# Seven half-size products for the FFN down projection and for the late gate/up pairs, with folded weights kept in DRAM

## The chip, the cores and the metric

The kernel runs on all 8 cores of one Trainium2 chip. Each core computes half of one of the four sequences, and no core waits for another. The metric is the device time of the slowest core, in microseconds (us). The fast executions of the kernel before took 5716.59 to 5722.73 us, but for one of 5781.71. More than half of the executions on record here (76 of the 126 listed with a state) fell into a slow state, whatever the kernel: the cores of one die, or both, show a lower granted TensorE clock, and the time is up to 20% longer (6875.58 us in the kernel before, with 0.812 to 0.816 on cores 0 to 3 and 0.998 to 0.999 on the others). I compare fast executions with fast ones, and stages with stages on cores at a granted clock of 0.98 or more, unless I say otherwise.

The engines of a core are named as in the profile: PE is TensorE, which runs the matmuls (PEld: its weight loads), DVE is VectorE, ACT is ScalarE, POOL is GpSimd, and SP is SyncE, which only issues DMAs here. PSUM is the memory that matmuls write to; the kernel divides its part of it (`ps`, 4096 float32 columns) into eight banks.

## The reference, cut to what matters

```python
D_MODEL, BATCH, SEQ, DEPTH, D_FF = 1024, 4, 8192, 4, 2816
def swiglu(h, w_gate, w_up, w_down):
    return (jax.nn.silu(h @ w_gate) * (h @ w_up)) @ w_down
def reference(x, ...):
    for i in range(DEPTH):
        h = rmsnorm(x, mix_pre_g[i])
        m = mixer_a(h, ...) if i % 2 == 0 else mixer_b(h, ...)   # gated MLP over chunks / causal pooling
        x = x + rmsnorm(m, mix_post_g[i])
        h = rmsnorm(x, ffn_pre_g[i])
        x = x + rmsnorm(swiglu(h, w_gate[i], w_up[i], w_down[i]), ffn_post_g[i])
    return x
```

Inputs are float32. The FFN, three products of 1024 by 2816 for every token and layer, is most of the work.

## The kernel before: the parts that matter

A core takes its tokens in five tiles (0 to 4). A tile has two halves of 384 to 512 columns (tokens), and goes through eight stages: mixer A, FFN, mixer B, FFN, and the same again for layers 2 and 3. Weights are stationary 128 by 128 blocks in bf16; each is used for one matmul per half. They come in pieces of 1 MB into a ring of six slots (`WR`) and are cast from float32 on the way by DMAs that POOL issues; DMAs that need no cast are issued by SP.

```python
def ffn_head(s, v, pi, pc):              # one gate/up pair (two of 22 feature blocks), one half
    # ... 4 banks of PSUM: (gate, up) x two feature blocks, 8 matmuls of v.n columns into each
    t_act(..., sg, bank(bg), AF.Silu)                                # ACT: silu(gate)
    t_dve(..., e.tensor_tensor(out=o, in0=bank(bu), in1=sg(), op=mult))   # DVE: times up

def chain(v, s, post, gpost, nxt, final=None):   # after a stage: post-norm, residual, next pre-norm
    def mult(fc): ... e.tensor_tensor(out=m, in0=m, in1=r, op=mult)           # m * rsqrt(...)
    def add(fc):  ... e.scalar_tensor_tensor(out=x, in0=m, scalar=g, in1=x)   # x += g * m
                  ... st.add(x)                                              # squares (ACT), sums (DVE)
    # ... eight chunks; then the ones-matmul (PE), rsqrt (ACT), and eight H = x * g * r (DVE)

# the FFN stage
pcs = [Piece(wf_gu[l, q]) for q in range(11)]
for pi in range(11):
    for h in hs:
        ffn_head(s, vout[h], pi, pcs[pi])
tp = [Piece(wf_dn[l, q]) for q in range(6)]
for h in hs2:
    out_proj(s, vlast[h], by_block(tp, NJ), NJ, ...)      # 22 x 8 matmuls of v.n columns
    chain(vlast[h], s, sts[h], ...)
```

`chain`: after the last matmul of a half, a serial string of DVE, ACT and PE operations must end before the next stage can start on that half. While it runs, PE has the other half to work on.

The order of instructions on each engine is fixed when the kernel is built: the program places every task with durations that it assumes, and each engine then runs its list in order. Both profiles show it: the instructions of DVE start in one order on all eight cores (4841 before, 6879 after), though at other times, and so do those of ACT, POOL, SP and PE's weight loads. That placement is a plan and not a measurement.

## Time and profile before

| | before |
|---|---|
| fast executions (same rounds as the changed kernel) | 5722.73, 5722.59, 5722.32 us |
| profiled execution (slowest core) | 5754.8 us |
| matmuls per core | 33311 |
| PE / DVE / ACT busy | 99% / 46% / 42% |

The page of the profile, slowest core: busy time with its share of the span, the traffic to memory, the chain of waits that ended last, and the largest group of instructions (line, engine, operation, out<-in, shape, count | busy us, mean ns | idle before, releaser).

```profile
PE 5696.8 (99%) x33311; PEld 3157.3 (55%) x33311; DVE 2630.8 (46%) x4841; ACT 2432.9 (42%) x5236; POOL 258.7 (4%) x492
...
HBM read 1082.53 MB, written 23.66 MB: 192 GB/s over the span
...
PE 94%; DVE 2%; DMA 1%; ACT 1%; issue 1%; another core or an unknown queue 0%; DVEq 0%; SPq 0%; ACTq 0%; POOLq 0%
...
L499 PE MATMUL ps<-H,WR 128*128 128x384 bf16 (+2 forms) x16640 | 2967.7, 338 | 11.8 <-ACT SQ L480 4.3
```

PE is busy 99% of the span and is 94% of the chain, and its largest group has next to no idle time before it (11.8 us beside 2967.7 busy). Undisturbed matmuls of N columns (128 to 512) start every N/2.4 + 2.5 ns on core 7 (medians of 56 ns at 128 columns, 162 at 384, 216 at 512). So PE bounds the kernel, and what can make it faster is fewer PE columns. (Core 1, the slowest of this profile, is on a die whose granted clock was at 0.81 for 149 to 262 us of the span; core 7, used below, is not, and PE is busy there for 5654.5 us.)

Three stretches of core 7 (an undisturbed die) follow: the first FFN of tile 0, mixer B of tile 1 and the FFN of layer 1 in tile 1. The columns are the stretch, its length, busy us of each engine with the count of instructions, the granted clock, the share of the DMA engines and GB/s.

```profile
core 7: us, PE busy (x) PEld busy (x) DVE busy (x) ACT busy (x) POOL busy (x), PEclk, DMA share, GB/s
164.87:349.34 184.47, 184.22 (x1101) 107.56 (x1100) 71.12 (x135) 62.61 (x126) 8.71 (x17) 1.00 0.70 126
1469.03:1525.31 56.28, 54.97 (x358) 28.20 (x357) 43.34 (x75) 41.41 (x89) 2.11 (x4) 1.00 0.51 93
1525.31:1725.89 200.58, 200.58 (x1062) 103.66 (x1060) 73.56 (x123) 59.05 (x111) 8.96 (x17) 1.00 0.47 85
```

In both FFNs PE is busy from end to end: 184.22 of 184.47 us and 200.58 of 200.58 us. What PE waited for in layers 1 to 3 of that tile (us in total, times, the longest):

```profile
PE ps L499 <- DVE H L641: 1.6, 2, 0.8
```

That is all that is listed in 867 us. What DVE, ACT and the DMA engines do is hidden.

### The profile page before, as it was taken

To read this page: it belongs to the slowest core of one execution; us is meant where nothing else is said; L and a number is where in the kernel's file an instruction comes from. 1 tells how busy PE (TensorE), PEld (TensorE's weight loads), DVE (VectorE), ACT (ScalarE), POOL (GpSimd) and SP (SyncE) were. 2 spreads that over 40 slices of the span, in tenths; PEclk is the share of its full clock that TensorE was granted. 3 is DMA by queue.
4 is the path that set the end of the run, shared out by engine and by line. 5 is a ranking of instruction groups with operands and counts; after the bars stand their busy time and mean duration, and the time that the engine had idled before them with its cause. 6 is when DMAs were issued, how large, how long until landed. Compare 5 with 4: busy or idle time off the path is not lost.

```text
span 5754.8 us, 92936 instructions; the slowest of 8 cores (5714.0 to 5754.8 us)
## 1 busy us (share of the span) xinstructions
PE 5696.8 (99%) x33311; PEld 3157.3 (55%) x33311; DVE 2630.8 (46%) x4841; ACT 2432.9 (42%) x5236; POOL 258.7 (4%) x492
## 2 busy tenths in 40 slices
PE   8999999999999999999999999999999999999999
PEld 4555555555555555555545555555565555555556
DVE  5453536352625454443436253524454444525352
ACT  5352635352525353533354253524534453525252
POOL 0000000000000000000000000000000000000000
PEclk9999999999999999999999999999999999999999
DMA  7856676664445545754544455655554676455544
GB/s 141 141 97 107 114 127 117 123 130 81 80 89 98 96 88 107 142 95 81 93 85 86 91 112 111 122 111 103 103 105 95 119 140 112 89 92 96 107 88 90
DMA packets 131409, 604.39 MB, mean 105 GB/s; under 512 B 12560, under 2 KB 55952, under 8 KB 67600
## 3 DMA queue, kind: packets, MB, share of 16 engines
q0 software_dynamic: 70272, 507.82, 51.1%
q1 hardware_dynamic: 60688, 90.63, 5.2%
q8 instruction: 276, 4.52, 0.3%
q14 instruction: 173, 1.42, 0.1%
HBM read 1082.53 MB, written 23.66 MB: 192 GB/s over the span
## 4 chain that ended last, share of the span: by engine, by line
PE 94%; DVE 2%; DMA 1%; ACT 1%; issue 1%; another core or an unknown queue 0%; DVEq 0%; SPq 0%; ACTq 0%; POOLq 0%
PE ps L499 94%; DMA MS<-xT 1%; DVE ACC L596 1%; DVE H L641 0%; DVE MS L688 0%; DMA WR<-wb_out 0%; ACT RS L622 0%; ACT BIG L480 0%; ACT RS L624 0%; DVE BIG L833 0%; DVE X L694 0%; ACT SQ L480 0%; DVE ACC L593 0%; ACT MS L480 0%; DMA X<-xT 0%
## 5 line engine op out<-in xcount | busy, mean ns | idle before, releaser
L499 PE MATMUL ps<-H,WR 128*128 128x384 bf16 (+2 forms) x16640 | 2967.7, 338 | 11.8 <-ACT SQ L480 4.3
L499 PEld LDWEIGHTS ps<-H,WR 128*128 128x128 bf16 x16640 | 1617.7, 98 | 1254.6 <-issue 24.7
L499 PE MATMUL ps<-BIG,WR 128*128 128x384 bf16 (+4 forms) x11056 | 1941.5, 337 | 2.1
L499 PEld LDWEIGHTS ps<-BIG,WR 128*128 128x128 bf16 x11056 | 1078.4, 98 | 832.8 <-issue 24.2
L750 DVE TENSOR_TENSOR BIG<-ps,SG 128x384 bf16<-128x384 f32 (+2 forms) x880 | 510.0, 585 | 1374.3 <-PE ps L499 1294.7
L480 ACT ACTIVATE SG<-ps 128x384 bf16<-128x384 f32 (+2 forms) x880 | 442.8, 513 | 1553.1 <-PE ps L499 1540.7
L596 DVE TENSOR_TENSOR ACC<-ACC,SQ 128x384 f32<-128x384 f32 (+2 forms) x730 | 428.7, 587 | 770.0 <-ACT SQ L480 706.7
L499 PE MATMUL ps<-WR,H 128*128 128x512 bf16 x3216 | 728.3, 386 | 12.8 <-DVE ACC L596 8.1
L480 ACT ACTIVATE MS<-ps 128x384 f32<-128x384 f32 (+3 forms) x648 | 324.5, 511 | 958.8 <-PE ps L499 947.6
L480 ACT ACTIVATE BIG<-ps 128x512 bf16<-128x512 f32 (+1 forms) x914 | 477.3, 561 | 338.2 <-PE ps L499 335.1
L499 PEld LDWEIGHTS ps<-WR,H 128*128 128x128 bf16 x3216 | 318.5, 99 | 402.7 <-issue 67.7
L688 DVE TENSOR_TENSOR MS<-MS,RS 128x384 f32<-128x384 f32 (+3 forms) x640 | 364.6, 580 | 200.0 <-ACT RS L624 199.9
L641 DVE SCALAR_TENSOR_TENSOR H<-X,GV,RS 128x384 bf16<-128x384 f32 (+2 forms) x576 | 330.0, 643 | 142.8 <-ACT RS L624 142.8
L480 ACT ACTIVATE SQ<-X 128x384 bf16<-128x384 f32 (+2 forms) x576 | 300.5, 549 | 200.9 <-DVE ACC L593 96.6
L694 DVE SCALAR_TENSOR_TENSOR X<-MS,GV,X 128x384 f32<-128x384 f32 (+2 forms) x560 | 354.6, 642 | 0.0
L480 ACT ACTIVATE SQ<-ps 128x384 bf16<-128x384 f32 (+3 forms) x648 | 321.9, 510 | 46.2 <-DVE ACC L596 29.2
L509 POOL DMA_DIRECT2D WR<-wf_gu x220 | 116.1, 528 | 2485.1 <-PE ps L499 2452.6
L593 DVE TENSOR_TENSOR ACC<-SQ 128x384 f32<-128x384 bf16 (+2 forms) x146 | 85.4, 585 | 189.4 <-ACT SQ L480 188.6
L480 ACT ACTIVATE SQ<-BIG 128x512 bf16<-128x512 bf16 x268 | 168.2, 638 | 7.1
L622 ACT ACTIVATE RS<-ps,EPSC 128x384 f32<-128x384 f32 (+2 forms) x152 | 92.6, 609 | 139.2 <-PE ps L499 139.1
L864 DVE SCALAR_TENSOR_TENSOR ACC<-ps,GV,BIAS 128x384 f32<-128x384 f32 (+2 forms) x184 | 107.5, 587 | 57.9 <-PE ps L499 54.8
L480 ACT ACT_TABLE_LOAD x94 | 120.6, 1283 | 19.7 <-PE ps L499 14.1
(63 smaller groups left out, 1555.9 us busy)
## 6 DMA issues: line engine op xcount, KB each, us to landing
WR<-wf_gu POOLq DMA_DIRECT2D x220, 1024.0 KB, 10.5
WR<-wf_dn POOLq DMA_DIRECT2D x120, 1024.0 KB, 9.0
WR<-wa_in POOLq DMA_DIRECT2D x79, 1024.0 KB, 14.3
WR<-wa_out POOLq DMA_DIRECT2D x40, 1024.0 KB, 10.0
WR<-wb_in POOLq DMA_DIRECT2D x20, 1024.0 KB, 10.1
WR<-w_s SPq DMA_DIRECT2D x20, 1024.0 KB, 10.2
yT<-MS SPq DMA_DIRECT2D x56, 192.0 KB, 16.6
X<-xT SPq DMA_DIRECT2D x48, 192.0 KB, 18.5
```

What stands on the lines that cost most here:

```text
L480: return e.activation(out=out() if callable(out) else out, in_=in_() if callable(in_) else in_, func=func, **kw)
L499: return e.matmul(out(), lhsT=lhsT() if callable(lhsT) else lhsT, rhs=rhs() if callable(rhs) else rhs, start=start, stop=stop)
L509: return e.dma_start(out=out() if callable(out) else out, in_=in_)
L593: t_dve(self.prio + (1,), lambda e: e.tensor_tensor(out=acc, in0=o0(), in1=o(), op=ALU.add), [k0, kq], ka, v.n)
L596: d = t_dve(self.prio + (1,), lambda e: e.tensor_tensor(out=acc, in0=acc, in1=o(), op=ALU.add), [kq] + ka, ka, v.n)
L622: t.insts.append((lambda e: e.activation(out=r, in_=bank(b, 0, v.n), func=AF.Ln, bias=EPSC[:]), [b, ("EPSC",)], kr, d_act(v.n)))
L641: t_dve(CH + (s, v.p, 1), lambda e, o=o, a=a, g=g, r=r: e.scalar_tensor_tensor(out=o, in0=a, scalar=g, in1=r, op0=ALU.mult, op1=ALU.mult), ...
L688: t_dve(CH + (s, v.p, 0), lambda e: e.tensor_tensor(out=m, in0=m, in1=r, op=ALU.mult), kf("MS", v, fc) + kr, kf("MS", v, fc), v.n)
L694: t_dve(CH + (s, v.p, 0), lambda e: e.scalar_tensor_tensor(out=o, in0=m, scalar=g, in1=x, op0=ALU.mult, op1=ALU.add), kf("MS", v, fc) + kf ...
L750: t_dve((0, s, v.p), lambda e, o=o, sg=sg, bu=bu: e.tensor_tensor(out=o, in0=bank(bu, 0, v.n), in1=sg(), op=ALU.mult), [bu, ksg], ko, v.n)
L864: t_dve((0, s, v.p, 0), lambda e, b=b, o3=o3, bb=bb, lg=lg, x0=x0, nl=nl, n=n: e.scalar_tensor_tensor(out=o3, in0=bank(b, x0 - v.c0, nl * ...
```

## The change

The intent is to spend DVE time, which is to be had, in place of PE time. A product of two matrices cut into 2 by 2 blocks needs eight half-size products, or seven when sums of blocks are multiplied (Strassen). The sums of weight blocks ("folds") are made once, in tile 0, by DVE, and written to DRAM in bf16 (`gu_s`, `dn_s`); tiles 1 to 4 load them without a cast. The sums of activations are made by DVE each time. Tile 0 itself computes as before. The change does this for the down projection of layers 0 to 2 and for the last 4 or 6 of 11 gate/up pairs (`LATE`).

```diff
-FFN_PIECES = 17
+LATE = (7,5,7,5)                     # pairs from here on use seven products, by layer
 ...
+    gu_s = dram("gu_s", [4, 128, 55 * 1024], BF16, "Internal")
+    dn_s = dram("dn_s", [3, 2, 128, 154 * 128], BF16, "Internal")
 ...
+    def ffn_head7(s, v, pi, st7, i, keep):
+        m = v.n // 2
+        # ... seven products, 8 matmuls of m columns each, 3 PSUM banks; one ACT copy, two DVE adds
+        t_act(..., AF.Silu);  t_dve(..., op=ALU.mult)
+        # ...
+        t_dve(..., out=cc, in0=tb.broadcast, in1=z.both(0, 2 * m), op=ALU.subtract)     # 4m columns
+        t_act(..., AF.Silu);  t_dve(..., op=ALU.mult)
+        if keep:
+            g_sums(s, v, pi)          # three bf16 sums for the down projection
 ...
+    def stage(s, l, jobs, claimed):   # tile 0: fold into a staging unit, then store the unit
+        for fn, n, src, dsts in jobs:
+            var = Var(kind)           # one of 8 or 11 units of 256 KB in free SBUF and temporaries
+            t = Task("dve", (1, s));  t.alloc = var
+            # ... fn: one DVE sum or difference of two weight blocks
+            for c0, nn, dst, key in dsts:
+                t_dma("sp", (0, s), dst, unit()[:, c0:c0 + nn], [var] + region, [key], ...)
 ...
-            pcs = [Piece(wf_gu[l, q]) for q in range(11)]
+            if t > 0:
+                pcs = [Piece(wf_gu[l, q]) for q in range(LATE[l])]
+                units = Units(l)      # folded gate/up weights from gu_s
+                # ... ffn_head for pairs below LATE[l], ffn_head7 from there
+            else:
+                pcs = [Piece(wf_gu[l, q]) for q in range(11)]
+                if l % 2 == 0:
+                    fold_group(j, s)
+                for pi in range(11):
+                    for h in hs:
+                        ffn_head(s, vout[h], pi, pcs[pi])
+                    if pi >= LATE[l]:
+                        setup_gu(s, l, pi, pcs[pi], claimed)      # 5 folds and stores
+            if keep:
+                # ... down7: 4 calls of seven products, 22 matmuls of m columns each
+            else:
+                # ... out_proj as before
+                if t == 0 and l < 3:
+                    for q in range(6):
+                        setup_dn(s, l, q, tp[q], claimed)         # 5 folds, 7 or more stores
```

(The diff is cut to its core: buffers moved, the placement's model of DMA and ports, and the layout of other weights are left out.)

## The prediction

> All times mean the fast state. The profiled execution took 5754.8 us at a granted clock of 0.99 or more on all cores (cores' view); of the three timed runs one was fast (5722.73 us), two were 18 to 19% slower. I compare with 5722.73.
>
> **What bounds it.** TensorE. The page gives PE 99% busy, DVE 46%, ACT 42%; the chain that ended last is 94% PE matmuls, with waits of 1 to 2% each. In the trace matmuls start every N/2.4 + 2.5 ns: 216 ns at 512 columns, 163 at 384, 109 at 256, 62.5 at 144, 56 at 128, each with its own weight load. [...] this trace shows 56, so halving the columns costs only the fixed 2.5 ns. The columns alone are 5541 us at 2.4 GHz, the fixed parts 85, gaps and clock about 90. Only fewer columns can help.
>
> **Removed.** Seven half-size products replace eight in tiles 1 to 4 (896, 896, 768, 784 columns: 3344).
> - Down, 3 layers: 176 matmuls of n columns become 308 of n/2: 22 x 3344 columns less per layer, 92 us; 132 more matmuls per half cost 8. Net -84 us.
> - 20 late pairs over four layers: 32 matmuls of n become 56 of n/2: 4 x 3344 columns less per pair, 111 us; 24 more matmuls cost 10. Net -102 us.
> Together -186 us: 5537 if nothing new stalls PE.
>
> **Added, I think off the chain.**
> - DVE takes 465 ns from start to start at 384 columns. A late pair and half needs four such operations, one of 768 and, in layers 0 to 2, three bf16 sums: about 3.5 us (estimate) in 4.6 us of matmuls, against 0.9 before. DVE grows by about 900 us to some 3500 (60 to 65%).
> - Weights. A cast 1 MB load takes 5.8 us of all DMA engines (51.1% of the span over 508 MB), a bf16 MB about 3.3 (5.2% over 90.6 MB). Down now streams 15 MB of folded bf16 weights (one half twice) instead of 5.8 MB: about 50 us of DMA in 59 us of matmuls, with six slots, about 16 us of lead. This is the tightest place; DMA busy should rise there from 4-6 tenths to 7-9.
> - PSUM: a unit holds a bank pair and one more, of seven; products are interleaved so that silu and multiply (about 1 us) hide behind 24 matmuls (2 us).
> - Tile 0: folding on DVE (about 115 us) and stores; PE work unchanged.
>
> I add 20 us for new stalls, most at the start of down and in late pairs.
>
> **Prediction:** 5557 us, 2.9% faster; 80% range 5505 to 5635. Faster by over 2% (below 5608): 0.80; within 2%: 0.17; slower: 0.03. In the slow state, scaled, about 6600; the state itself I can't predict.
>
> **Right if:** about 7,000 more matmuls, those of 192 columns at 82 ns pitch; DVE near 60 to 65%; chain still over 90% PE; no wait of PE over 60 us in total.
> **Wrong if, most likely first:** PE waits on weight DMA in down (lead too short); PE waits on DVE or ACT for banks in late pairs; 192-column pitch above 85 ns; granted clock below 0.99 [...]; tile 0 longer because folding holds weight slots.

## The result, and the profile after

The ratio of two kernels is the mean time of one kernel's fast executions over the mean of the other's fast executions of the same rounds, so it is not quite the ratio of the medians that I quote. Executions in which one die ran at a lower clock are left out of the means.

| | before | after |
|---|---|---|
| fast executions, us | 5722.73, 5722.59, 5722.32 | 5746.66, 5732.89 |
| ratio of fast executions | | 1.003 (95%: 1.0005 to 1.0054) |
| profiled span, slowest core | 5754.8 | 5745.1 |
| matmuls | 33311 | 40319 |
| PE / DVE / ACT busy | 99% / 46% / 42% | 96% / 60% / 44% |

I had predicted 5557 us. The page after:

```profile
PE 5524.3 (96%) x40319; PEld 3645.5 (63%) x40319; DVE 3453.2 (60%) x6879; ACT 2501.6 (44%) x5356; POOL 200.1 (3%) x380
...
HBM read 1135.48 MB, written 80.15 MB: 212 GB/s over the span
...
PE 82%; DMA 7%; ACT 4%; DVE 3%; issue 2%; SPq 1%; DVEq 0%; ACTq 0%; POOLq 0%
...
L557 PE MATMUL ps<-H,WR 128*128 128x384 bf16 (+5 forms) x14080 | 2333.7, 322 | 81.8 <-ACT SG L530 38.0
```

The number of matmuls rose by 7,008. Put at N/2.4 + 2.5 ns each, the pitch in both traces (82.5 ns at 192 columns in the new one), the recorded matmuls of core 7 sum to 5624.3 us before and 5438.4 after: the saving of 186 us was there. (The busy time of PE on the two pages fell by 172 us, but these are different cores and the one before was disturbed; on core 7 it fell by 130 us, from 5654.5 to 5524.3, because some matmuls after gaps ran slower, 427 ns at 512 columns instead of 216, as shown below.) But the span hardly moved, the chain is only 82% PE, and there is idle time before the matmuls on `H` (81.8 us, of which the largest part, 38.0, for ACT; before it was 11.8). The writes to memory rose from 23.66 to 80.15 MB: the 56 MB of folded weights.

Where the time went shows by tile. I take the start of the first matmul of each stage, counted in program order; the length of a stage is the median over the cores with complete records (before: of the die at clock 0.998 or more; after: all at 0.988 or more), and a tile is the sum of its stages. Tile 0 includes the 21 us before the first stage.

```
                    before     after
tile 0              1118.4    1200.7     +82.3
tile 1              1220.0    1194.9     -25.1
tile 2              1220.2    1196.1     -24.1
tile 3              1051.6    1026.7     -24.9
tile 4              1093.8    1067.7     -26.1
tiles 1 to 4        4585.6    4485.4    -100.2
```

So two things went wrong. Tile 0, for which I expected nothing, lost 82 us. Tiles 1 to 4, for which I expected a gain of 186 us less some stalls, gained 100. By stage, the loss of tile 0 lies in its four FFNs: 184.5, 174.0, 180.7 and 182.3 us before, 213.5, 190.3, 199.2 and 194.5 after. The cores of one execution differ: tile 1 starts at 1172 to 1210 us in this profile, so a difference of 15 us in tile 0 between two runs is not clear of that spread. (The slowest core, 7, is about 40 us over the median. In tiles 1 to 4 PE waited 27 us there for the mixers' weights and DVE 11.6 us for one late reload of mixer A's bias, which cores 0 to 5 don't show; and core 7 had the most time at half clock, 140.5 us against 76.8 to 135.7 on the others, more on that below.)

The same three stretches of core 7 as before:

```profile
167.27:384.88 217.61, 190.52 (x1103) 108.77 (x1102) 104.09 (x192) 63.73 (x129) 8.97 (x17) 0.95 0.88 183
1548.66:1606.41 57.75, 54.78 (x359) 28.40 (x356) 42.29 (x74) 40.20 (x86) 2.11 (x4) 1.00 0.59 121
1606.41:1800.68 194.27, 187.35 (x1614) 147.88 (x1612) 132.83 (x268) 67.73 (x122) 4.22 (x8) 0.99 0.52 149
```

The first FFN of tile 0 takes 217.61 us instead of 184.47. PE is busy for only 190.52 of them, though the matmuls are the same in number; DVE works 104.09 us instead of 71.12 and the DMA engines are taken for 0.88 of the time instead of 0.70. Layer 1's FFN of tile 1 takes 194.27 us, of which PE is busy 187.35; it was 200.58 and all busy.

**Tile 0.** What DVE waited for on the stores of folded weights (all of these lie in tile 0; L1098 is the fold, for gate/up through `setup_gu`, L1130 for down):

```profile
DVE TB L1098 <- DMA gu_s<-TB: 40.2, 6, 27.8
...
DVE BIG L1098 <- DMA gu_s<-BIG: 34.7, 11, 6.5
...
DVE TB L1130 <- DMA gu_s<-TB: 23.3, 4, 17.5
...
DVE BIG L1130 <- DMA gu_s<-BIG: 16.2, 2, 16.0
```

With 14 us more for stores of `dn_s`, DVE stood 128 us before folds whose staging unit still held a fold that had not landed in DRAM. One such moment, the last gate/up folds of layer 3, in three views of the timeline (start, duration, engine, line, operation, count, [idle before <- releaser]): SP's issues, DVE, PE.

```profile
1062.15 40.06 SPq L567 DMA_DIRECT2D gu_s<-BIG  x8
```

```profile
1105.62 0.69 DVE L1098 TENSOR_TENSOR TB<-WR 128x1024 bf16<-128x1024 bf16 x1 [27.82 <-DMA gu_s<-TB]
...
1107.43 0.55 DVE L880 TENSOR_TENSOR BIG<-ps,SG 128x384 bf16<-128x384 f32 x1
```

```profile
1079.84 9.91 PE L557 MATMUL ps<-H,WR 128*128 128x384 bf16 x60
1108.71 7.61 PE L557 MATMUL ps<-H,WR 128*128 128x384 bf16 x34 [18.96 <-ACT SG L530]
```

These eight stores and three more, all eleven staging units of the layer, were issued from 1061 to 1103 us; in the trace they all land between 1105.5 and 1111.8 us, the first of them 44 us after its issue. The issuing itself was slow: the eight took SP 40 us, where the median issue of a `gu_s` store took 0.32. DVE stands 27.82 us before the fold into `TB`, which has to wait for one of them. Behind that fold in DVE's list is the multiply that frees PSUM banks (L880). ACT stands for a buffer that this multiply would free (20.3 us in one wait), and PE stands 18.96 us for ACT. Nothing passed the fold on DVE in those 27.82 us. By the start times of the packets, the stores land just when the cast loads of the stage run out: the last packet of the loads starts at 1103.7 us.

How long the stores take, by the page's table of DMA issues (KB each, median us from issue to landing):

```profile
gu_s<-BIG SPq DMA_DIRECT2D x72, 256.0 KB, 11.8
...
dn_s<-BIG SPq DMA_DIRECT2D x37, 256.0 KB, 10.8
...
gu_s<-TB SPq DMA_DIRECT2D x28, 256.0 KB, 14.4
```

The placement assumed some 6 us; the medians are 10 to 14 us and the longest 44.

**Boundaries in tiles 1 to 4.** What PE waited for in layers 1 to 3 of tile 1, beside 1.6 us before:

```profile
PE ps L557 <- DVE H L727: 10.2, 4, 2.6
PE ps L557 <- ACT SG L530: 3.4, 2, 1.7
PE ps L557 <- DVE SQ L660: 2.6, 3, 1.7
PE ps L557 <- ACT SQ L530: 1.8, 2, 0.9
```

With two shorter ones these are 20 us in one tile, most of them on the norm chain (`SQ`, `H`) of the stage before. The start of layer 1's FFN in tile 1, PE and then DVE:

```profile
1606.41 1.63 PE L557 MATMUL ps<-H,WR 128*128 128x384 bf16 x9
...
1633.69 2.80 PE L557 MATMUL ps<-MS,WR 128*128 128x192 bf16 x32
1638.20 0.38 PE L557 MATMUL ps<-SQ,ONESM 128*128 128x512 bf16 x1 [1.70 <-DVE SQ L660]
1641.08 7.03 PE L557 MATMUL ps<-H,WR 128*128 128x512 bf16 x24 [2.51 <-DVE H L727]
```

```profile
1629.83 0.74 DVE L795 SCALAR_TENSOR_TENSOR X<-MS,GV,X 128x512 f32<-128x512 f32 x1
...
1637.37 0.68 DVE L660 TENSOR_TENSOR SQ<-ACC,SQ 128x512 bf16<-128x512 f32 x1
1637.97 0.35 DVE L843 TENSOR_TENSOR BIG<-BIG 128x384 bf16<-128x384 bf16 x1
...
1640.18 2.08 DVE L727 SCALAR_TENSOR_TENSOR H<-X,GV,RS 128x512 bf16<-128x512 f32 x3
```

The stage's first matmul starts at 1606.41 us, and PE works on the first half (`H`, 384 columns, and 32 narrow products) until 1636.49. Next in its list is the second half, which waits for the last residual add (L795, at 1629.83), the sum of its squares (L660, at 1637.37), the matmul with ones (1638.20) and the scaled `H` (L727, at 1640.18). DVE's sums for the seven products (L843 and its neighbours) run in between. The same place in the kernel before, DVE and then PE:

```profile
1554.81 2.08 DVE L641 SCALAR_TENSOR_TENSOR H<-X,GV,RS 128x512 bf16<-128x512 f32 x3 [2.46 <-ACT RS L624]
```

```profile
1555.71 8.58 PE L499 MATMUL ps<-H,WR 128*128 128x512 bf16 x39
```

There the stage starts at 1525.31 us, and PE turns to the second half at 1555.71, after 30.4 us; `H` starts to come at 1554.81, after 29.5 us. So the chain was hidden with less than a microsecond to spare. After the change PE still has 30.1 us of work for the first half, but `H` comes 33.8 us after the start of the stage: the chain has become later by 4.3 us, on a DVE that has more to do.

The gap costs more than itself. The granted clock in stretches of the same moment (the third column from the right is PEclk):

```profile
1641.00:1645.20 4.20, 4.12 (x12) 1.51 (x13) 4.20 (x7) 0.00 (x0) 0.00 (x0) 0.59 0.00 0
...
1650.00:1660.00 10.00, 9.89 (x47) 4.44 (x47) 3.39 (x8) 1.33 (x3) 0.00 (x0) 1.00 0.10 16
```

For 4 us after the gap, PE runs at a clock of 0.59 on average; matmuls of 512 columns start every 427 ns there instead of every 216. The trace has the clock at half from 1641.71 us, for 3.41 us; before that, PE had stood idle in gaps of 1.70 and 2.51 us that one 0.38 us matmul parts. Core 7 has 20 such stretches, 140.5 us in all (3 and 18.2 us before the change); on the eight cores there are 131, and in the 7 us before each of them PE was idle for 1.8 to 5.4 us. Over core 7, gaps of over 0.35 us rose from 36 to 204 us, and matmuls that started more than 20% later than their usual pitch cost 75 us instead of 29.

### The profile page after: what moved, and what is told of

Its sections match the earlier page's. It is cut to its first block, busy times and chain, and to the rows that moved or that the text cites. A ratio compares the mean times of both kernels' runs of the same rounds, so it can differ in the third digit from the quotient of the medians.

```text
span 5745.1 us, 110595 instructions; the slowest of 8 cores (5670.8 to 5745.1 us)
## 1 busy us (share of the span) xinstructions
PE 5524.3 (96%) x40319; PEld 3645.5 (63%) x40319; DVE 3453.2 (60%) x6879; ACT 2501.6 (44%) x5356; POOL 200.1 (3%) x380
## 3 DMA queue, kind: packets, MB, share of 16 engines
HBM read 1135.48 MB, written 80.15 MB: 212 GB/s over the span
## 4 chain that ended last, share of the span: by engine, by line
PE 82%; DMA 7%; ACT 4%; DVE 3%; issue 2%; SPq 1%; DVEq 0%; ACTq 0%; POOLq 0%
PE ps L557 82%; DMA WR<-wa_in 2%; DMA WR<-wb_in 1%; DMA gu_s<-TB 1%; DMA gu_s<-BIG 1%; SPq L567 1%; DVE H L727 1%; ACT SQ L530 1%; DMA w_s<-BIG 1%; ACT L530 1%; DMA BIG<-bias_s 1%; ACT BIG L530 1%; ACT RS L682 1%; DVE ACC L654 0%; ACT MS L530 0%
## 5 line engine op out<-in xcount | busy, mean ns | idle before, releaser
L557 PE MATMUL ps<-H,WR 128*128 128x384 bf16 (+5 forms) x14080 | 2333.7, 322 | 81.8 <-ACT SG L530 38.0
L557 PEld LDWEIGHTS ps<-H,WR 128*128 128x128 bf16 x14080 | 1336.2, 98 | 944.0 <-issue 134.3
L557 PE MATMUL ps<-BIG,WR 128*128 128x384 bf16 (+6 forms) x14224 | 1843.3, 291 | 15.1 <-DVE BIG L880 10.6
L557 PEld LDWEIGHTS ps<-BIG,WR 128*128 128x128 bf16 x14224 | 1299.3, 98 | 526.9 <-issue 37.5
L557 PE MATMUL ps<-MS,WR 128*128 128x192 bf16 (+2 forms) x6400 | 609.3, 253 | 0.0
L557 PEld LDWEIGHTS ps<-MS,WR 128*128 128x128 bf16 x6400 | 557.7, 98 | 24.7 <-issue 1.6
L530 ACT ACTIVATE MS<-ps 128x384 f32<-128x384 f32 (+4 forms) x552 | 274.2, 509 | 685.9 <-PE ps L557 682.7
L727 DVE SCALAR_TENSOR_TENSOR H<-X,GV,RS 128x384 bf16<-128x384 f32 (+2 forms) x576 | 330.9, 641 | 131.1 <-ACT RS L684 130.0
L795 DVE SCALAR_TENSOR_TENSOR X<-MS,GV,X 128x384 f32<-128x384 f32 (+2 forms) x560 | 352.4, 638 | 0.0
L876 DVE TENSOR_TENSOR BIG<-ps,SG 128x384 bf16<-128x384 f32 (+2 forms) x304 | 176.2, 589 | 273.8 <-PE ps L557 270.2
L959 DVE TENSOR_TENSOR TB<-ps,TB 128x384 f32<-128x384 f32 (+2 forms) x416 | 245.1, 589 | 73.4 <-PE ps L557 40.7
L880 DVE TENSOR_TENSOR BIG<-ps,SG 128x384 bf16<-128x384 f32 (+2 forms) x256 | 142.7, 565 | 216.1 <-PE ps L557 196.2
L530 ACT ACTIVATE SQ<-ps 128x384 bf16<-128x384 f32 (+4 forms) x456 | 222.2, 506 | 57.5 <-DVE ACC L654 33.9
```

What stands on the lines that cost most here:

```text
L530: return e.activation(out=out() if callable(out) else out, in_=in_() if callable(in_) else in_, func=func, **kw)
L557: return e.matmul(out(), lhsT=lhsT() if callable(lhsT) else lhsT, rhs=rhs() if callable(rhs) else rhs, start=start, stop=stop, skip_group_ ...
L727: t_dve(CH + (s, v.p, 1), lambda e, o=o, a=a, g=g, r=r: e.scalar_tensor_tensor(out=o, in0=a, scalar=g, in1=r, op0=ALU.mult, op1=ALU.mult), ...
L795: t_dve(CH + (s, v.p, 0), lambda e: e.scalar_tensor_tensor(out=o, in0=m, scalar=g, in1=x, op0=ALU.mult, op1=ALU.add), kf("MS", v, fc) + kf ...
L876: t_dve((0, s, v.p), lambda e, o=o, sg=sg, bu=bu: e.tensor_tensor(out=o, in0=halved(bank(bu, 0, v.n)), in1=halved(sg()), op=ALU.mult), [bu ...
L880: t_dve((0, s, v.p), lambda e, o=o, sg=sg, bu=bu: e.tensor_tensor(out=o, in0=bank(bu, 0, v.n), in1=sg(), op=ALU.mult), [bu, ksg], ko, v.n)
```

## The experiments

Seventeen kernels ran. "Tile 0" and "tiles 1 to 4" are read as in the table above; the diffs are against the changed kernel unless I say otherwise. "Q" in the later expectations is the theory that the stores starve behind the casting loads in the DMA engines; "P" its rival that the number of packets alone counts; "B" is the theory that the stalls of tiles 1 to 4 sit at stage boundaries.

| run | result | fast executions, us | tile 0 | tiles 1 to 4 |
|---|---|---|---|---|
| before | right | 5722.3 to 5722.7 | 1118.4 | 4585.6 |
| after | right | 5732.9, 5746.7 | 1200.7 | 4485.4 |
| e1_no_fold | wrong | 5665.2, 5671.8 | 1128.6 | 4493.9 |
| e2_fold_no_store | wrong | 5648.4 | 1121.8 | 4491.6 |
| e3_store_tail | right | none (lowest 5779.4) | 1142 and 1198 | |
| e4_down_only | right | 5748.7, 5775.7 | 1158 to 1250 | |
| e5_narrow_store | right | 5743.2 | 1207.1 | 4488.6 |
| e6_wide_store | right | 5707.7 to 5720.7 | 1190.3 | 4487.0 |
| e7_late_7777 | right | 5734.8 | 1186.8 | 4503.6 |
| e8_wide_late_7676 | right | 5705.9 | 1185.4 | 4501.2 |
| e9_paced | right | 5679.3, 5688.6, 5701.0 | 1158.6 | 4487.0 |
| e10_paced_wide_7676 | right | 5702.4, 5705.1 | 1168.2 | 4501.0 |
| e11_paced4_7676 | right | none (lowest 5756.6) | 1170.2 | 4495.5 |
| e12_best | right | 5653.3 to 5665.9 (five) | 1148.6 | 4475.1 |
| e13_paced_no_dn_store | wrong | 5652.8 | 1122.3 | 4488.1 |
| e14_short_chain | wrong | 5680.9 | 1192.4 | 4428.6 |
| e15_before_short_chain | wrong | 5716.1 to 5717.5 | 1117.1 | 4582.9 |
| e16_two_rings | right | 5668.3, 5690.2, 5724.6 | 1155.7 | 4474.9 |
| e17_two_rings_only | right | 5729.0, 5737.6 | 1215.3 | 4487.0 |

### What makes tile 0 longer: folds or stores?

**e1_no_fold.** The folded weights come as an input (unfolded numbers, so the result is wrong); nothing is folded or stored.

```diff
-    gu_s = dram("gu_s", [4, 128, 55 * 1024], BF16, "Internal")     # dn_s the same
+    gu_s = dram("gu_s", [4, 128, 55 * 1024], BF16)
     def setup_gu(s, l, pi, pc, claimed):                           # setup_dn the same
+        return
```

> Wrong result on purpose: the folded weights come in ready as an input (plain bf16 casts of other weights), so tile 0 neither folds nor stores; all else as after. In the trace of after the eight stages of tile 0 took about 1179 us against 1099 before (median of cores), tiles 1 to 4 about 107 us less than before. All theories that put the loss on folding (S: DVE stands in line behind a fold that waits for a store to land; C: the fold arithmetic itself on DVE; W: folds hold weight slots; D: stores take DMA bandwidth) expect tile 0 at 1090 to 1110 us and the whole at 5640 to 5670 us, 70 to 90 us under after. If the new order of weights and banks is to blame instead, tile 0 stays near 1180 us.

Measured: ratio 0.9908 to the kernel before (0.9865 to 0.9951), tile 0 at 1128.6 us. (The expectations of e1 to e4 count the eight stages alone, without the first 21 us: by that count 1106.9 us here and 1100.2 in e2, both as expected.) So folding with its stores costs some 70 us in tile 0.

**e2_fold_no_store.** The same, but DVE folds into its staging units and only the stores are left out (wrong).

```diff
             for c0, nn, dst, key in dsts:
-                t_dma("sp", (0, s), dst, ...)
+                pass
```

> Wrong result on purpose: as e1, but DVE does fold in tile 0, into the same staging units; nothing is stored. S and D (stores) expect the same as e1 within 10 us, tile 0 at 1090 to 1115 us. C and W (arithmetic, slots) expect tile 0 at 1160 to 1180 us, as after.

Measured: tile 0 at 1121.8 us, whole 5648.41 us. The DVE work of folding is next to free (tile 0 took 1118.4 us before the change), and so is holding weight slots until the folds are done. The stores are the cost: 79 us of the changed kernel's 1200.7. (The down weights' direct stores, which hold a slot until they land, are left out here too, so their hold on slots counts with the stores.) (One fast execution; it is the profiled one, and every core's clock was good.)

**e3_store_tail.** The placement is told that a store takes 10 us more.

```diff
-                      128 * nn * 2, (csem, var))
+                      128 * nn * 2, (csem, var)).tail = 10.0
```

> Right result. The same work as after; the static scheduler is told that a store of folded weights takes 10 us longer to land (it assumed about 6 us; the trace of after shows medians of 11 to 14 us for 256 KB), so it places folds later on DVE. S expects most of the loss back: DVE waits on stores fall from about 128 us to under 40, tile 0 at 1100 to 1130 us, the whole 40 to 80 us under after. D and W expect no change over 15 us, since traffic and slots are the same.

Inconclusive: no execution was fast, and on the two cores whose clock was not lowered in tile 0 it took 1142 and 1198 us. Planning for slow stores alone is not enough.

**e4_down_only.** No gate/up pair uses seven products, so only `dn_s` is stored.

```diff
-LATE = (7,5,7,5)
+LATE = (11,11,11,11)
```

> Right result. Seven products for the FFN down alone, no late pairs, no folded gate/up weights. By my sum down alone saves 84 us of matmuls in tiles 1 to 4. If the folding of gate/up (100 of the 190 folds, and the ones with the long DVE waits in the trace) makes most of the 80 us of tile 0, tile 0 falls to 1100 to 1130 us and the whole lands at 5640 to 5680 us, faster than after. If the down folds make the loss, tile 0 stays at 1150 us or more and the whole is at 5700 us or more.

A miss: 5748.69 us at best, ratio 1.0072 (0.997 to 1.0174, so unclear), tile 0 at 1158 to 1250 us on the less disturbed die (clock 0.974 to 0.979) of a slow profile. DVE still waited 67 us on stores of `dn_s`. Fewer stores didn't help in proportion.

### Why are the stores slow?

The folded weights of one FFN of tile 0 compete with its cast loads. I counted the packets of the two queues in slices of 5 us between 160 and 1150 us (core 7 of the changed kernel; a slice counts as shared when each queue starts more than 60 packets in it, as alone when the other starts fewer than 10 or 5):

```
                         loads (q0, 8 KB each)     SP's queue (q1, mean 2 KB)
59 slices shared         16.5 packets per us       23.4 packets per us
37 slices, loads alone   19.4                      0
25 slices, q1 alone      0                         135.2
mean time of a packet in the shared slices: 823 ns and 98 ns
```

A queue that could do 135 packets per us gets 23 while a load is in line, and the loads give up 15%. The mean of 23.4 holds slices in which the loads pause: in the median slice SP's queue starts 1.06 packets for each packet of the loads (a quarter of the slices are under 0.97, a quarter over 1.27). So about one small row starts for each large one, which takes eight times as long (823 ns and 98 ns); in what order the DMA engines take the rows, the trace doesn't show. An estimate from these numbers, for layer 1 of tile 0: 17 load pieces of 128 packets take 132 us at 16.5 per us; its 79 stores (30 of gate/up, 49 of down) of 128 packets are 10,100 packets, of which 3,100 go out beside the loads and the others need 52 us more: 184 us, over the whole length of that FFN (174 us before). There is no slack left.

**e5_narrow_store.** Every gate/up store as two of 1 KB rows: twice the packets, the same bytes.

```diff
-                         1024, [pc.var], [(0, 1024, d, key)]))
+                         1024, [pc.var], [(0, 512, d[:, 0:512], key), (512, 512, d[:, 512:1024], key + (1,))]))
```

> Right result. As after, but each store of a folded gate/up unit (256 KB, 128 rows of 2 KB) is two stores of 128 rows of 1 KB: the same bytes, twice the packets. Theory P ([...] in the trace of after, while cast weight loads of 8 KB packets stand in the POOL queue, the SP queue gets one 2 KB packet for each of theirs, 80 against 80 in 5 us) expects the loss in tile 0 (79 us over e2's 1122) to grow to 110 to 170 us, tile 0 at 1230 us or more. Theory D (bytes, bandwidth) expects tile 0 at 1200 us, as after, within 15.

Tile 0 at 1207.1 us, only 6 us more than the changed kernel. A miss for the theory that the number of packets alone decides. The ratio itself stayed: 1.11 of SP's packets, now mostly of 1 KB, for each of the loads in the median slice (1.03 in e6). So the rate beside the loads is not what sets the loss in proportion, and theory Q does not explain this run.

**e6_wide_store.** Two staging units next to each other go out as one store with 4 KB rows: half the packets.

```diff
+            if wide_dst is not None and len(parts) > 1:
+                dsts = [(0, 2 * n, wide_dst(...), [p[3][0][3] for p in parts])]
```

> Right result. As after, but two folded gate/up units are staged side by side and stored as 128 rows of 4 KB: the same bytes, three stores instead of five per pair. P expects the loss in tile 0 to fall from 79 us to 15 to 45 us (tile 0 at 1137 to 1167 us), and the whole to come to 5680 to 5720 us fast. D expects tile 0 unchanged at 1200 us. Tiles 1 to 4 unchanged in both.

Tile 0 at 1190.3 us, 10 us less, and short of what I expected. The whole ran at 5707.7 to 5720.7 us, ratio 0.9987 (0.9968 to 1.0007). Wide units come free later, which takes back part of what fewer packets give; that reason is only argued.

**e9_paced.** A load piece of tile 0 may only start when the stores of the pair three before it have landed. The number and size of packets stay. One more thing moves, which the cut leaves out: mixer B's own weight fold comes after the pairs instead of before them, in layers 0 and 2.

```diff
-                pcs = [Piece(wf_gu[l, q]) for q in range(11)]
+                def stored(pi):
+                    return [("gus", l, 5 * pi + o) for o in range(5)] if LATE[l] <= pi < 11 else []
                 for pi in range(11):
+                    pc = Piece(wf_gu[l, pi], reads=stored(pi - 3))
 ...
-                tp = [Piece(wf_dn[l, q]) for q in range(6)]
+                tp = [Piece(wf_dn[l, q], reads=stored(11 - 3 + q) if t == 0 else []) for q in range(6)]
```

> Right result. The same work, stores and staging as after; only the weight loads of tile 0 are paced: the load of pair p waits until the folded units of pair p-3 have landed in DRAM (the first pieces of the down likewise). Theory Q: stores starve because cast loads run ahead into all six slots and keep the POOL queue full for 30 to 40 us; [...] stores land in bursts at the end, DVE stands in front of a fold that waits for its unit, and TensorE starves. Q expects store landings of 30 to 45 us to disappear (maximum under 20 us), DVE waits on stores under 40 us (after: about 128), tile 0 at 1125 to 1160 us (after 1200, without stores 1122), and the whole 5650 to 5690 us fast. The rival (stores cost bandwidth or DVE time wherever they stand) expects tile 0 at 1185 us or more, or longer because loads come later.

Tile 0 at 1158.6 us, half of the loss gone. That it is the pacing shows in the FFNs of layers 1 and 3, where nothing else moved: 174.3 and 180.4 us instead of 190.3 and 194.5, what they take without any store (174.3 and 179.5 in e2). The whole ran at 5679.31 us at best, ratio 0.9923 (0.9805 to 1.0041, so unclear; one fast execution of the kernel before was 5781.71 us, which widens it). DVE's longest waits on stores, core 7:

```profile
DVE BIG L1130 <- DMA dn_s<-BIG: 32.7, 8, 23.2
...
DVE TB L1130 <- DMA dn_s<-TB: 15.9, 2, 15.2
...
DVE BIG L1098 <- DMA gu_s<-BIG: 8.5, 2, 4.3
```

All waits on `gu_s` fell from 114 to 18 us, those on `dn_s` rose from 14 to 49. Two finer points of the expectation missed: the waits are 67 us in all, not under 40, and on core 7 stores still landed up to 29 us (`gu_s`) and 45 us (`dn_s`) after their issue. So loads that run ahead were what held up the stores; and what paced loads leave are the stores of the down weights.

**e10_paced_wide_7676** and **e11_paced4_7676** vary this: with wide stores, and with a distance of four pairs, each with `LATE = (7,6,7,6)`.

```diff
-LATE = (7,5,7,5)
+LATE = (7,6,7,6)
-                    pc = Piece(wf_gu[l, pi], reads=stored(pi - 3))
+                    pc = Piece(wf_gu[l, pi], reads=stored(pi - 4))        # e11 alone
```

> Right result. Paced loads, wide stores (two units, 4 KB rows) and seven products after 7, 6, 7, 6 pairs. If Q holds, tile 0 at 1120 to 1150 us, tiles 1 to 4 as e8 (about 4500), the whole 5630 to 5675 us fast, ratio to before 0.984 to 0.992.

> Right result. Loads paced at a distance of four pairs instead of three, stores as after (2 KB rows), 7, 6, 7, 6. Q expects a weaker cure than distance three, since four loads may be in line: store landings up to 30 us, tile 0 at 1135 to 1175 us, the whole 5650 to 5695 us.

Neither was better, and e10 missed its range for tile 0: 1168.2 and (undisturbed die) 1170.2 us; 5702.38 us for the first at best, ratio 0.9946 (0.9832 to 1.006); no fast execution of the second.

**e13_paced_no_dn_store.** Paced as e9, with the down weights loaded from an input and their stores dropped. The folds stay, other than the expectation says: DVE still makes all 90 of them, and nothing reads them.

```diff
+                if key[0] == "gus":
                     t_dma("sp", (0, s), dst, ...)
 ...                                              # the two direct stores of setup_dn are dropped too
```

> Folded down weights come as an input, so DVE neither stores nor folds them (same bytes loaded later); gate/up folds and stores paced as in e9_paced; result stays right. If the rest of tile 0's loss after pacing (1158.6 us in e9_paced against 1120.4 before) is the down folds' stores, tile 0 is at most 1135 us and DVE's waits on dn_s are gone. If it is the gate/up stores that remain, or the paced loads themselves, tile 0 stays at 1150 or above.

Tile 0 at 1122.3 us: what it takes with no stores at all (e2) and 4 us more than before the change. Since the folds are still made, the rest of the loss is the down stores. My note that the result stays right was a mistake: I gave unfolded numbers in their place, so it is wrong. The time doesn't rest on that.

**e17_two_rings_only.** The direct test of the one row for each row of the loads, and of whether a second queue gets as much: every second store is issued by ACT, whose DMAs go through a queue of their own (q10). Nothing is paced.

```diff
+    def ring(key):
+        return "act" if (key[2] if key[0] == "gus" else key[3]) % 2 else "sp"
-                t_dma("sp", (0, s), dst, ...)
+                t_dma(ring(key), (0, s), dst, ...)
```

> Correct result. The changed kernel with one edit: every second store of folded weights is issued by ACT, on a queue of its own, instead of SP; no pacing; static plan unchanged (5564.7 us). Theory Q ([...] stores on one queue get half of the packets beside the cast loads, and stores on two queues two thirds): stores and loads in a busy 5 us show about 2 packets of stores per packet of cast load instead of 1; gu_s and dn_s land with a median of 7 to 10 us and a maximum under 32 instead of 11 to 14 and 44; DVE's waits on those stores fall from 128 us to under 80; tile 0 at 1150 to 1175 us instead of 1200; whole 5690 to 5720 in the fast state. If the stores' total over the engines is limited by something else (writes to DRAM), two queues share the same 20 packets per us, landings stay as they are, and tile 0 stays at 1190 or above.

The queues (packets, MB, share of the engines' time), and then ACT's two longest waits for folds in tile 0:

```profile
q0 software_dynamic: 54144, 390.37, 38.7%
q1 hardware_dynamic: 105296, 408.90, 20.7%
q10 hardware_dynamic: 16272, 26.09, 1.4%
```

```profile
ACT SG L530 <- DVE TB L1101: 26.3, 3, 21.4
ACT BIG L530 <- DVE TB L1133: 21.5, 2, 20.6
```

In the 50 slices in which all three queues started more than 40 packets, they started 15.0 (loads), 23.8 (SP) and 24.0 (ACT) packets per us. So a second queue does get rows of its own: beside the loads the stores' rate doubled, from 23.4 to 47.8 packets per us, and the loads gave up only a tenth. The other half of the expectation failed. Tile 0 took 1215.3 us, 15 more than the changed kernel. DVE's waits on stores fell only to 106 us, and ACT, which never waited for a fold before, by its list of waits, now stands in its own list before stores whose fold is late: 84 us in four such groups. The rate beside the loads rose as expected; more rows beside the loads were not worth another in-order engine tied to the folds.

### What holds PE at the boundaries of tiles 1 to 4?

**e7_late_7777.** Layers 1 and 3 use fewer late pairs, so that PE has longer work at the start of the stage.

```diff
-LATE = (7,5,7,5)
+LATE = (7,7,7,7)
```

> Right result. As after, but layers 1 and 3 too turn to seven products only after seven pairs (not five): 2 x 8 fewer late pair-halves, about 2.5 us of matmuls more in each FFN of layers 1 and 3. Theory B: with five early pairs TensorE runs out of work for the first half at the boundary from mixer to FFN, and waits for the second half's norm (idle 7.5 us in the trace of after in each such stage, nearly as the static schedule itself foresaw). B expects the FFN of layer 1 in tiles 1 and 2 at 187 to 190 us (after: 195), of layer 3 at 195 to 197 (after: 199.5). Rival: if the late pairs themselves saturate DVE, the gain is less than the 2.5 us of matmuls that are lost: 194 us or more in layer 1.

Layer 1's FFN in tile 1 took 193.0 us instead of 194.6, short of the 187 to 190 expected, though it has more matmul work. Idle time fell there by some 4 us. But the reload of mixer A's bias came late in tile 4 (DVE waited 2 to 14 us for it, by core). Partial support.

**e8_wide_late_7676.** Wide stores and `LATE = (7,6,7,6)`.

> Right result. Wide stores and seven products after 7, 6, 7, 6 pairs: the candidate to beat both. If P and B hold, tile 0 at 1135 to 1165 us and tiles 1 to 4 about 10 us under after; the whole at 5660 to 5705 us fast, a ratio to before of 0.988 to 0.997. If neither holds, 5730 us as after.

Layer 1's and 3's FFNs in tile 1 took 191.6 and 195.7 us (194.6 and 199.6 in the changed kernel), and tile 4 gave it back: 1087.5 us instead of 1067.7. 5705.89 us in the one fast execution; tile 0, at 1185.4 us, missed its range.

**e14_short_chain.** In tiles 1 to 4 (all stages but the very first) the post-norm multiply covers 16 columns instead of all (wrong), which takes eight DVE operations of about 0.58 us out of each chain.

```diff
+            w = 16 if s > 8 else v.n
-            t_dve(CH + (s, v.p, 0), lambda e: e.tensor_tensor(out=m, in0=m, in1=r, op=ALU.mult), ...
+            t_dve(CH + (s, v.p, 0), lambda e: e.tensor_tensor(out=m[:, :w], in0=m[:, :w], in1=r[:, :w], ...
```

> Wrong result on purpose: in tiles 1 to 4 the post-norm multiply (eight DVE operations per half and stage) covers 16 columns instead of the half's 384 to 512; all else is as in the changed kernel, tile 0 too. Theory B (at the boundaries after down and before the mixers PE waits for the second half's norm chain, which is longer than the first half's shortened tail of matmuls): the FFNs of layers 1 and 3 in tiles 1 and 2 fall from 194.6 and 199.6 to 187 to 190 and 193 to 196, the mixers B from 57.7-59.4 to 54 to 56, tiles 1 to 4 together 35 to 55 us shorter, whole 5690 to 5715 in the fast state with tile 0 unchanged near 1200. Rival (the stall is in the late pairs' banks or DVE sums, not the norm chain): under 10 us in tiles 1 to 4.

The same two stretches (mixer B and layer 1's FFN, tile 1), and PE's waits of layers 1 to 3:

```profile
1527.43:1582.31 54.88, 54.52 (x359) 28.31 (x356) 35.28 (x74) 40.21 (x86) 2.11 (x4) 1.00 0.61 116
1582.31:1768.90 186.59, 185.43 (x1613) 147.46 (x1612) 125.55 (x268) 67.33 (x122) 4.22 (x8) 1.00 0.52 157
```

```profile
PE ps L557 <- ACT SQ L530: 1.8, 2, 0.9
...
PE ps L557 <- DVE H L727: 0.2, 1, 0.2
```

The mixer falls from 57.75 to 54.88 us and the FFN from 194.27 to 186.59, with the same matmuls; the wait for `H` falls from 10.2 us to 0.2. `H` of the second half now comes 28.3 us after the start of the stage (from the timeline), in time again. Tiles 1 to 4 together take 4428.6 us, 57 less than the changed kernel: the upper end of what theory B expected. The whole took 5680.85 us, with tile 0 at 1192.4 as it was.

**e15_before_short_chain.** The control: the same edit in the kernel before (wrong).

> Control, wrong result on purpose: the same edit in the kernel before. If the norm chain was fully hidden before (theory B says the change uncovered it), the time is that of the kernel before, 5715 to 5730 us in the fast state, ratio 0.998 to 1.002. If the chain cost time before as well, it is 20 us or more faster.

5716.09 to 5717.52 us, ratio 0.9995 (0.9976 to 1.0015). The chain cost nothing before: the eight operations that cost the changed kernel 57 us were hidden. One detail of theory B falls, at least at the boundary shown above: the first half's work was not shorter (30.1 us against 30.4), the chain was later.

### A version that beats both

**e12_best.** Paced loads (with mixer B's own weight fold after pair 7), `.tail = 10.0` for down stores, and late pairs from 6 in layers 1 and 3 of tiles 1 and 2 only.

```diff
-                      128 * nn * 2, (csem, var))
+                      128 * nn * 2, (csem, var)).tail = 10.0 if key[0] == "dns" else 0.0
+                late = 6 if t < 3 and l % 2 else LATE[l]
 ...                                              # and the edit of e9_paced
```

> Correct result. The paced weight loads of e9_paced (distance 3 pairs), the down stores given 10 us more in the static placement, and late pairs from pair 6 instead of 7 in layers 1 and 3 of tiles 1 and 2 only (in tiles 3 and 4 that edit made the bias reload late). Theory Q (the stores starve behind cast loads that run ahead): tile 0 at 1140 to 1165 us, median of the fast cores, as e9_paced or a little better. Theory B (boundary stalls): FFN of layers 1 and 3 in tiles 1 and 2 2 to 4 us shorter each than in the changed kernel (194.6 and 199.6). Whole: 5660 to 5690 us in the fast state, ratio to the kernel before 0.989 to 0.995. If pacing was luck of the schedule, tile 0 is over 1175 and the whole over 5700.

All held, the whole at or below its range: 5653.34 to 5665.90 us in five fast executions, ratio 0.9896 to the kernel before (0.9879 to 0.9914), tile 0 at 1148.6 us, the two FFNs in tile 1 at 191.7 and 195.6 us. It is 1.0% faster than the kernel before, with an interval clear of 1. It didn't run in the same rounds as the changed kernel, whose fast executions were at 5733 and 5747 us.

**e16_two_rings.** e12_best with the two queues of e17.

> Correct result. e12_best (paced loads, down stores planned 10 us longer, late pairs from 6 in layers 1 and 3 of tiles 1 and 2) with every second store of folded weights on ACT's queue. Theory Q: tile 0 falls from e12_best's 1148.6 us to 1130 to 1142, DVE's remaining waits on stores (about 27 us in e12_best) go nearly to zero; whole 5635 to 5660 in the fast state, ratio to the kernel before 0.986 to 0.990. If ACT now stands before stores whose fold is late, tile 0 is as in e12_best or longer.

A miss: 5668.27, 5690.15 and 5724.59 us, ratio 0.9955 (0.9838 to 1.0073), tile 0 at 1155.7 us. The expectation's last sentence came true.

## Why the prediction was wrong, point by point

- **The saving in matmuls: right.** I predicted some 7,000 more matmuls and 186 us less work. The count rose by 7,008, and matmuls of 192 columns start 82.7 ns apart (82 predicted); the work of the recorded matmuls fell by 186 us. I had taken the pitch from the trace before (56 ns at 128 columns), and it held in the new code.
- **DVE's load: right.** 60% predicted at the lower end, 60% measured (3453.2 us, against "some 3500").
- **Weight streaming in down: my first worry, not it.** PE's waits on weight DMA in tiles 1 to 4 are about 27 us in core 7 (2 to 10 in cores 0 to 5), for the mixers' weights (`wa_in`, `wb_in`) and not for `dn_s`.
- **The step that failed first: "Tile 0: folding on DVE (about 115 us) and stores; PE work unchanged."** The work was unchanged, the time was not: 82 us instead of none. I costed the DVE arithmetic (which e2 shows to be next to free: 1121.8 us) and not the landing of the stores. Their rate beside cast loads is a sixth of what it is alone (23.4 packets per us against 135.2), DVE stands in its list before the next fold, and PE behind DVE. e2 (no stores: 1121.8 us), e9 (paced loads: 1158.6) and e13 (no down stores either: 1122.3) show this; e17 shows that a second queue gets as much again (47.8 packets per us in all), but by these rates alone e5 and e17 should have moved tile 0 much more than they did (1207.1 and 1215.3 us against 1200.7), so how the landings turn into lost time is only partly settled. My list had tile 0 last among the risks, and for the slots, which was the wrong reason.
- **The step that failed second: "I add 20 us for new stalls, most at the start of down and in late pairs."** Tiles 1 to 4 gained 100 us of 186. The stalls are at the start of a stage, where PE is ready for the second half before its norm chain has ended; for the late pairs' own adds and copies PE waited 1 us in core 7. The plan that the kernel makes when it is built could have told: rebuilt from the two kernels, it takes 4584.3 us for tiles 1 to 4 before and 4446.2 after, a gain of 138 and not 186, so 48 us of new stalls, more than the 20 I added, stood in the plan before any run. e14 gives 57 us of the 86 back by a shorter chain, and e15 shows that the chain cost nothing before. e14 takes load off DVE as well as length off the chain, so the two aren't parted. The other 29 us are not settled; waits for mixers' weights are among them.
- **The sum.** 186 us saved, 82 lost in tile 0, 86 in the stalls of tiles 1 to 4: about 18 us gain in the median core, and the slowest core gives that back. I had named "chain still over 90% PE" and "no wait of PE over 60 us in total" as signs of being right; the chain was 82% PE, and gaps were 204 us in core 7. The granted clock did fall below 0.99 on three cores (0.988 to 0.989), but by half clock after gaps (77 to 141 us of each core's span), with no time at 0.81.

## What to carry to other kernels

Behind an engine that was 99% busy everything else was hidden here, but at one boundary with 0.9 us to spare: before loading a second engine, look in the timeline how much slack each chain between stages has, and not just whether that engine's average has room. Preparation that is done once still stands in the lists of in-order engines: a store that freed its buffer late held DVE, and all that stood behind the next use of that buffer, for 27.82 us. Small plain stores beside large casting loads got about one row for each row of the loads here (1.06 at the median); where the stores have a deadline, hold the loads back (e9: tile 0 at 1158.6 us instead of 1200.7), since changing the stores' rows (e5: 1207.1, e6: 1190.3) or queues (e17: 1215.3) did little.
